# Second feed-forward product: sums in the places of blocks that are read no more, the late block in two buffers, operand loads over two groups, x1 of the tail in halves

## The chip, the cores and the metric

The kernel runs on one core of a Trainium2 chip. The metric is the device time of one execution in microseconds: before the change the median of three runs is 2979.29 us (2977.74 to 2981.48). Times inside an execution come from the hardware profiler's trace of one further execution; they count from its first instruction. Engines are named as in the profile: PE is TensorE, DVE VectorE, ACT ScalarE, POOL GpSimd, SP SyncE. SP and POOL issue DMAs here; each has its own queue.

## The reference, cut to what matters

The reference is one inference step of a one-layer encoder for T = 576 tokens (512 of a prompt, 64 of a sample) with D = 2048. After a token mixer that leaves x1, the change touches the feed-forward part:

```python
def conv_ffn(h, conv_prev, lp):
    ...
    up = h @ lp['w_up']
    ...
    out = (jax.nn.gelu(a_conv) * bv) @ lp['w_down']
...
f, conv_new = conv_ffn(h2, conv_prev, lp)
x = x + rms_norm(f, lp['norm_post_ffn'])
```

Here `w_up` is 2048 x 11264 and `w_down` 5632 x 2048, all in float32. The second product, gelu(a) * b times `w_down`, is called the down product below; its 5632 rows are the gated hidden channels.

## The kernel before, in words

**Float32 in three passes.** A weight block of 128 x 1024 numbers is loaded into a buffer `raw` (SP), cast into `wh` (ACT, L148: the high part, in a type that TensorE takes at full pace), and the rest raw - wh is written into `wl` by a subtraction (DVE, L160; every second block of the last eight on POOL). The operand has two parts too, `xh` and `xl`, prepared the same way and kept in DRAM (`gcd`). A product is three matmuls: wh with xh, wh with xl, wl with xh.

**One list of blocks.** All weight blocks stand in one list and `go(i)` works on block i. In the last parts of the kernel it issues loads some blocks ahead (`dma_to`), sees to the subtraction of block i + 1 (`l_to`), then the evacuations that the block before has left in `late`, then sums and the cast of block i + 2 (`h_to`), and last the 24 matmuls of block i. Each engine runs its own instructions in this order, and each DMA queue issues in its order too; an instruction that must wait holds everything behind it on its engine.

**The down product (L1530, PE).** 5120 of the 5632 rows are cut into five chunks, the 2048 columns into four quarters: 20 groups, number n = 4 * chunk + quarter. A group is a 2 x 2 block product by a seven-product scheme: weight blocks A11, A12, A21, A22 and sums of them, against seven operand combinations kept in SBUF (`E`, `xh`, `xl`, high and low halves). A group therefore has seven positions of 24 matmuls. In the order of work the weights are: A11; A12; A11 + A21 + A22; A21 + A22; A11 + A21; A11 + A12 + A21 + A22 combined in `ws1`; A22. Five of the sums are made by DVE (`tt`, L1537), all into two buffers `ws0` and `ws1`; the third position takes two sums, one on the other's result, made in a row ahead of its cast.

**Banks.** Three PSUM banks are used in a group, in the order A, B, A, C, A, C, A. The third position cannot start until the first one's bank has been evacuated into `f` (DVE, L1537; in chunk 0 four of the seven on ACT, L1960), the fourth use waits for the third, and so on.

**Loads.** A11, A21, A12 come into the three rotating `raw` buffers, in SP's queue. A22, the late block, has one buffer of its own; SP loads it (`w_load`, L1911) when the block at position 5 has been handed to PE. The operands of the next chunk lie in the other half of the SBUF operand buffers: 14 loads of 576 KB (`ring_load`, L1885), issued by POOL. In program order they stand in the second group of a chunk, high and low half of an operand together, but they wait only for the last matmul that reads what they overwrite, and that is in the last group of the chunk before: that is when they run.

**The up product's end.** The last group of the up product ends in `down_open`, which makes the last gating (two products on DVE and their stores), closes the buffers of the up product, opens those of the down product (`f`, `ws`) and issues the first load of A22.

**The tail (L1993).** The last 512 rows are a plain product of 16 blocks, eight for tokens 256 to 575 and eight for tokens 0 to 255. Between them `tail_square` collects squares, `tail_turn` (L2089) transposes and scales, and `tail_out` (L2131, `scalar_tensor_tensor` on DVE) adds x1 and stores. x1 comes from DRAM (`x1td`) in six loads on POOL's queue, all in `tail_start` (L2049, L2051).

Of the kernel before, what the change touches and what calls it, by code (L numbers as in the profile page):

```python
# [36 lines left out]
def kernel(ctx: ExitStack, tc: tile.TileContext, I: dict, O: dict):  # L37
# [1440 lines left out]
    def ffn_open():  # L1478
        M3["cm"].__exit__(None, None, None)
        rbc_.__exit__(None, None, None)  # L1480
        extra["pool"] = None
        F["ecm"] = tc.tile_pool(name="pe", bufs=1, reuse_waits="tile")
        F["ep"] = F["ecm"].__enter__()
        F["E"] = F["ep"].tile([P, 2, 3, 8, HT], F32R, tag="E", name="E")
        F["cm"] = tc.tile_pool(name="p4", bufs=1, reuse_waits="tile")
        p = F["cm"].__enter__()
        F["p"] = p
        extra.update(pool=p, n=2, kind=2, turn=4)
# [4 lines left out]
        F["a2"] = [p.tile([P, 578], F32, name="a%d" % j) for j in range(2)]  # L1493
# [4 lines left out]
        F["xt"] = p.tile([P, T], F32, name="xtok")  # L1498
        for k in range(2):
            x_load(k)  # L1500
# [53 lines left out]
    def x_step(p, n):  # L1554
# [5 lines left out]
        if n == 1:  # L1560
            tt(a0, a0, a1, ALU.subtract)
            tt(a1, b1, a1, ALU.subtract)
        elif n == 2:
            stt(b1, a0, -1.0, b1, ALU.subtract)
            nc.scalar.copy(E[:, 0, 0:2, p, :], x2)
        elif n == 3:
            stt(b0, b1, -1.0, b0, ALU.subtract)
            nc.scalar.copy(E[:, 0, 2, p, :], b1)
        elif n == 4:
            gh = F["gh", "x"] = F["p"].tile([P, T], F32R, tag="gh", name="gh", bufs=2)  # L1570
            nc.scalar.copy(gh[:, 0:HT], b0)
            nc.scalar.dma_start(x4d[0, :, p], gh[:, 0:HT].bitcast(F32))
            low(E[:, 1, 0:2, p, :], x2, E[:, 0, 0:2, p, :])
        elif n == 5:
            low(E[:, 1, 2, p, :], b1, E[:, 0, 2, p, :])
        elif n == 6:
            gl = F["p"].tile([P, T], F32R, tag="gl", name="gl")
# [184 lines left out]
    def xtok(k, step):  # L1762
# [19 lines left out]
        elif step == 5:  # L1782
            xo = F["p"].tile([P, T], F32, tag="gh", name="xo", bufs=2)
# [3 lines left out]
    def up_group(q, part):  # L1787
# [24 lines left out]
        def run(j):  # L1812
            def run_(h, lo):
# [37 lines left out]
                if last:  # L1851
                    ring_load(0, SEVEN[j])
                    if j == 3:
                        conv_last()
                    if j == 6:
                        while late:
                            late.pop(0)()
                        down_open(q)
# [8 lines left out]
    def conv_last():  # L1867
# [4 lines left out]
        co = F["p"].tile([P, T], F32, tag="gh", name="co", bufs=2)  # L1872
# [8 lines left out]
    def ring_load(c, o):  # L1881

        for hl in range(2):
# [6 lines left out]
    def down_open(q):  # L1890
# [5 lines left out]
        F["cm"].__exit__(None, None, None)  # L1896
        evp_.__exit__(None, None, None)
        extra["pool"] = None
        F["cm"] = tc.tile_pool(name="p5", bufs=1, reuse_waits="tile")
        F["p"] = F["cm"].__enter__()  # L1900
        F["f"] = [F["p"].tile([P, 4, T], F32, name="f%d" % m) for m in range(4)]
        F["ws"] = [F["p"].tile([P, 1024], F32, name="ws%d" % m) for m in range(2)]
        F["A22"] = stage_w["t"][2].bitcast(F32)
        w_load(F["A22"], 0, 0, 1, 1)
# [4 lines left out]
    def w_load(dst, c, mq, m, e):  # L1909

        nc.sync.dma_start(  # L1911
# [4 lines left out]

    def down_group(c, mq):
        R = {}

        def ld(name, m, e):  # L1920
            def load(alloc):
                R[name] = alloc()
                w_load(R[name], c, mq, m, e)
            return load

        def add(j, a, b):
            def src():
                g = lambda x: F["ws"][x] if isinstance(x, int) else F["A22"] if x == "A22" else R[x]
                tt(F["ws"][j], g(a), g(b), ALU.add)
                return F["ws"][j]  # L1930
            return src

        def two_sums():
            add(0, "A21", "A22")()
            return add(1, 0, "A11")()

        srcs = [lambda: R["A11"], lambda: F["ws"][0], two_sums, lambda: R["A12"],
                add(0, "A11", "A21"), add(1, 1, "A12"), lambda: F["A22"]]
        loads = [ld("A11", 0, 0), None, ld("A21", 1, 0), ld("A12", 0, 1), None, None, None]

        def run(j):
            def run_(h, lo):
# [29 lines left out]
        for j in (0, 3, 2, 1, 4, 5, 6):  # L1972
            block(1024, loads[j], run(j), srcs[j], 3)
# [4 lines left out]
    def last_run(a, mb):  # L1978
# [61 lines left out]
    def tail_start():  # L2040
# [11 lines left out]
        nc.scalar.activation(F["sp"].tile([P, 2], F32), ones, AF.Sqrt)  # L2052
# [82 lines left out]
    def tail_end():  # L2135
# [5 lines left out]
        F["cm"].__exit__(None, None, None)  # L2141
        F["ecm"].__exit__(None, None, None)
# [8 lines left out]
    def go(i):  # L2151
# [4 lines left out]
        else:  # L2156
            up = i < N_DOWN
            dma_to(i + 9 if i < N_DOWN - 9 else min(i + 9, N_DOWN + 6) if up else i + 7 if i < N_TAIL else i + 4)
# [3 lines left out]
            if up:  # L2162
                s_to(min(i + 3, N_DOWN))
                h_to(min(i + 2, N_DOWN))
# [89 lines left out]
```

## Time and profile before

| what | value |
|---|---|
| median of three runs | 2979.29 us (2977.74 to 2981.48) |
| the profiled execution's own time | 2983.06 us |
| its span, first to last instruction | 2981.3 us |
| mean granted TensorE clock | 0.984 |
| PE busy | 2847.2 us |
| DVE busy | 1844.2 us |
| ACT busy | 1171.7 us |
| POOL busy | 547.7 us |
| up product's last stretch | 1851.86 to 2339.71 us |
| down product | 2349.50 to 2885.80 us |
| tail | 2885.80 to 2981.30 us |

A window row gives the stretch, its length, the busy time and number of instructions of PE, PEld (weight loads into the array), DVE, ACT and POOL, then the granted clock, the busy share of the DMA engines and GB/s. A timeline row gives start, duration, engine, line, operation and tiles, and in brackets the idle time before it with what ended it. In the wait view a row gives the total, the number and the longest. "issue" is idle time for which the profile shows no cause. Matmuls overlap, so a matmul's duration of some 0.29 us is longer than the distance between two starts.

### The profile page before, as it was taken

What the parts mean: (1) busy time and instruction counts of PE and PEld (TensorE: products, weight loads), DVE (VectorE), ACT (ScalarE), POOL (GpSimd) and SP (SyncE); (2) the same over time, 40 slices, a digit from 0 to 9 for tenths busy, and PEclk for the clock granted to TensorE, in tenths of its full rate; (3) what the DMA queues carried; (4) which work ended last, traced back from release to release, by engine and by line L of the source; (5) the groups of instructions that cost most, each with busy time, mean ns of one, the idle gap of its engine ahead of it and who ended that gap; (6) DMA issues with size and microseconds to landing.
All of it is one profiled execution on the core that took longest, in us unless ns stands there. A gap on an engine that the chain in (4) does not pass through costs nothing.

```text
span 2981.3 us, 51790 instructions
## 1 busy us (share of the span) xinstructions
PE 2847.2 (96%) x21387; PEld 2783.9 (93%) x21387; DVE 1844.2 (62%) x2585; ACT 1171.7 (39%) x1764; POOL 547.7 (18%) x619
## 2 busy tenths in 40 slices
PE   8999999999999999998899999999999797898987
PEld 7999999999999999988899999999999797898986
DVE  7424533435252233378888888888888566676766
ACT  4322422222222234455555555555555342222223
POOL 2200010133330004454121211100000300110105
PEclk9999999999999999999999999999999899999998
DMA  8732343344343335574655554544544943543353
GB/s 272 195 79 68 83 129 81 99 112 113 98 115 98 96 120 156 163 234 158 196 161 155 175 164 147 160 136 128 160 137 126 321 143 132 196 164 110 117 162 129
DMA packets 519532, 431.51 MB, mean 145 GB/s; under 512 B 62844, under 2 KB 472114, under 8 KB 517952
## 3 DMA queue, kind: packets, MB, share of 16 engines
q1 hardware_dynamic: 467296, 298.42, 34.6%
q0 software_dynamic: 25792, 97.30, 9.5%
q10 hardware_dynamic: 26208, 32.48, 3.1%
q8 instruction: 168, 2.75, 0.4%
q14 instruction: 68, 0.56, 0.1%
HBM read 343.94 MB, written 84.90 MB: 144 GB/s over the span
## 4 chain that ended last, share of the span: by engine, by line
PE 80%; DVE 9%; DMA 4%; issue 3%; ACT 2%; POOL 1%; SPq 0%; ACTq 0%; DVEq 0%; POOLq 0%
PE ps L1530 37%; PE ps L199 36%; DVE wl L160 3%; DVE ws L1537 2%; DMA wl<-in_w_down_dram 2%; PE ps L224 2%; ACT wh L148 2%; DVE f L1537 1%; PE ps L327 1%; PE ps L1993 1%; DVE xl L1400 1%; DMA raw<-in_w_down_dram 1%; PE ps L1070 0%; PE ps L1074 0%; PE ps L622 0%
## 5 line engine op out<-in xcount | busy, mean ns | idle before, releaser
L160 DVE TENSOR_TENSOR wl<-raw,wh 128x1024 fp32r<-128x1024 f32 (+2 forms) x406 | 489.3, 1206 | 352.9 <-ACT wh L148 227.4
L1530 PE MATMUL ps<-E,wh 128*128 128x288 f32 x2880 | 589.2, 299 | 71.0 <-issue 32.4
L199 PE MATMUL ps<-xh,wl 128*128 128x288 f32 x2944 | 642.9, 296 | 13.7 <-DVE wl L160 13.7
L199 PE MATMUL ps<-xh,wh 128*128 128x288 f32 x2944 | 651.6, 299 | 3.7 <-DVE r_ss L1366 1.9
L199 PE MATMUL ps<-xl,wh 128*128 128x288 f32 x2944 | 641.7, 296 | 3.2 <-DVE xl L1400 3.2
L148 ACT CAST wh<-raw 128x1024 fp32r<-128x1024 f32 (+2 forms) x398 | 399.2, 1003 | 529.1 <-PE ps L199 290.2
L1530 PE MATMUL ps<-xh,wh 128*128 128x288 f32 x1920 | 569.4, 297 | 6.0 <-DVE f L1537 4.9
L1530 PE MATMUL ps<-xh,wl 128*128 128x288 f32 x1920 | 565.3, 294 | 0.7 <-DVE wl L160 0.7
L1530 PE MATMUL ps<-xl,wh 128*128 128x288 f32 x1920 | 565.1, 294 | 0.0
L1530 PEld LDWEIGHTS ps<-E,wh 128*128 128x128 f32 x2880 | 469.0, 191 | 74.7 <-issue 51.0
L199 PEld LDWEIGHTS ps<-xh,wl 128*128 128x128 f32 x2944 | 478.5, 189 | 16.0 <-DVE wl L160 15.8
L199 PEld LDWEIGHTS ps<-xh,wh 128*128 128x128 f32 x2944 | 476.8, 189 | 16.7 <-issue 9.9
L199 PEld LDWEIGHTS ps<-xl,wh 128*128 128x128 f32 x2944 | 478.2, 189 | 4.7 <-DVE xl L1400 4.7
L1530 PE MATMUL ps<-E,wl 128*128 128x288 f32 x1440 | 428.2, 297 | 0.4 <-DVE wl L160 0.4
L1530 PEld LDWEIGHTS ps<-xh,wh 128*128 128x128 f32 x1920 | 360.2, 188 | 9.6 <-issue 8.0
L1530 PEld LDWEIGHTS ps<-xh,wl 128*128 128x128 f32 x1920 | 360.2, 188 | 1.0 <-DVE wl L160 1.0
L1530 PEld LDWEIGHTS ps<-xl,wh 128*128 128x128 f32 x1920 | 360.3, 188 | 0.0
L1530 PEld LDWEIGHTS ps<-E,wl 128*128 128x128 f32 x1440 | 275.2, 191 | 1.0 <-DVE wl L160 1.0
L160 DVE TENSOR_TENSOR wl<-sums,wh 128x1024 fp32r<-128x1024 f32 x160 | 196.0, 1225 | 49.9 <-PE ps L1530 47.4
L148 ACT CAST wh<-ws 128x1024 fp32r<-128x1024 f32 x80 | 82.2, 1047 | 300.4 <-DVE ws L1537 277.2
L148 ACT CAST wh<-sums 128x1024 fp32r<-128x1024 f32 x160 | 168.2, 1051 | 62.7 <-PE ps L1530 59.6
L160 DVE TENSOR_TENSOR wl<-ws,wh 128x1024 fp32r<-128x1024 f32 x80 | 97.9, 1224 | 77.3 <-ACT wh L148 67.7
(464 smaller groups left out, 3037.0 us busy)
## 6 DMA issues: line engine op xcount, KB each, us to landing
raw<-in_w_up_dram SPq DMA_DIRECT2D x180, 512.0 KB
raw<-in_w_in_dram SPq DMA_DIRECT2D x118, 512.0 KB
raw<-in_w_down_dram SPq DMA_DIRECT2D x60, 512.0 KB
gcd<-gh ACTq DMA_DIRECT2D x62, 288.0 KB
E<-gcd POOLq DMA_DIRECT2D x30, 576.0 KB, 8.9
gd<-ev SPq DMA_DIRECT2D x48, 288.0 KB
gate<-gd SPq DMA_DIRECT2D x48, 288.0 KB
gcd<-wl POOLq DMA_DIRECT2D x40, 288.0 KB, 3.0
```

The costliest lines, as they stand in the source:

```text
L148: (nc.vector.tensor_copy if 4 <= i < KD else nc.scalar.copy)(as_src(raws[i], h, n), raws[i])
L160: E.tensor_tensor(out=out, in0=raw, in1=hi, op=ALU.subtract)
L199: mm(ps[:, a, 0:HT], w[:, c0:c0 + P], x[:, a * HT:(a + 1) * HT], start=start and i == 0, stop=stop and i == 2,)
L224: nc.tensor.transpose(out, in_, ident[0:k, 0:k])
L327: mm(mps[t][:, a, :], x[:, c], w[:, a * 512:(a + 1) * 512], start=k == 0 and i == 0, stop=k == KD - 1 and i == 2)
L1400: nc.vector.scalar_tensor_tensor(out=xl[:, k, c], in0=x1[:, c], scalar=gcol[:, G_FFN, k:k + 1], in1=xh[:, k, c].bitcast(F32), op0=ALU.mult ...
L1530: mm(bank, w[:, c0:c0 + P], x, start=start and p == 0 and i == 0, stop=p == n - 1 and i == 2, skip_group_check=True)
L1537: nc.vector.tensor_tensor(out=out, in0=a, in1=b, op=op)
L1993: mm(ps[:, j, 0:n], w[:, c], x, start=k == 0 and i == 0, stop=k == 3 and i == 2)
```

## The change

- **Sums in place.** Four sums a group instead of five, each made as soon as its inputs are there: at position 0 A11 += ws0 (ws0 holds A21 + A22), at position 2 ws0 = A11 + A12 (with what A11 has become), at position 5 ws0 = A21 + A22 of the next group, at position 6 A21 += A11 of the next group. Group 0 makes its first three at position 0. A sum stands behind the subtraction and the evacuations of its step.
- **The late block in two buffers**: the old one and `ws1`, alternating. The first A22 is loaded on POOL's queue during the last group of the up product.
- **Loads by name**: A22 of the next group at position 1, A21 and A11 at position 2, A12 at position 3, into buffers that are held, A21 and A12 swapping theirs from group to group.
- **Operand loads over two groups**: the high halves stand in the second group of a chunk, the low halves in the third.
- **The up product's end** is split: `down_open` opens only what the first group needs, and `up_close` makes the last gating at position 3 of the first group.
- **The tail**: a third `wl` buffer, subtractions one block earlier, the first raw blocks loaded in the last group, x1 in ten halves, one a block.

The core of the diff:

```diff
-        if kind < 2:
+        if kind < 2 or kind == 4:
             return wp.tile([P, 1024], F32R, tag="wl", name="wl", bufs=3)
...
                 if last:
+                    if j == 0:
+                        w_load(stage_w["t"][2].bitcast(F32), 0, "A22", nc.gpsimd)
                     ring_load(0, SEVEN[j])
...
-        F["f"] = [F["p"].tile([P, 4, T], F32, name="f%d" % m) for m in range(4)]
+        F["f"] = [F["p"].tile([P, 4, T], F32, name="f0")]
         F["ws"] = [F["p"].tile([P, 1024], F32, name="ws%d" % m) for m in range(2)]
-        F["A22"] = stage_w["t"][2].bitcast(F32)
-        w_load(F["A22"], 0, 0, 1, 1)
+        F["A22"] = (stage_w["t"][2].bitcast(F32), F["ws"][1])
...
+    def w_buf(n, name):
+
+        if name == "A22":
+            return F["A22"][n % 2]
+        return R5[0 if name == "A11" else 1 + n % 2 if name == "A21" else 2 - n % 2]
+
+    def down_sums(n, pos):
+
+        def s1(n):
+            tt(F["ws"][0], w_buf(n, "A21"), w_buf(n, "A22"), ALU.add)
+
+        def s3(n):
+            tt(w_buf(n, "A21"), w_buf(n, "A21"), w_buf(n, "A11"), ALU.add)
+
+        if pos == 0:
+            if n == 0:
+                s1(0)
+                s3(0)
+            tt(w_buf(n, "A11"), w_buf(n, "A11"), F["ws"][0], ALU.add)
+        elif pos == 2:
+            tt(F["ws"][0], w_buf(n, "A11"), w_buf(n, "A12"), ALU.add)
+        elif n + 1 < 4 * NCH and pos > 4:
+            (s1, s3)[pos - 5](n + 1)
+
+    def down_loads(n, pos):
+
+        if n + 1 < 4 * NCH:
+            for name in {1: ("A22",), 2: ("A21", "A11"), 3: ("A12",)}.get(pos, ()):
+                w_load(w_buf(n + 1, name), n + 1, name)
+        elif pos in (2, 3):
+            dma_to(N_TAIL + pos - 1)
...
-                if j == 5 and (c, mq) != (NCH - 1, 3):
-                    n = c * 4 + mq + 1
-                    w_load(F["A22"], n // 4, n % 4, 1, 1)
-                if mq == 1 and (c + 1 < NCH or j in (0, 3, 5, 6)):
-                    ring_load(c + 1, SEVEN[j])
+                down_loads(n, DOWN_ORDER.index(j))
+                if mq in (1, 2) and (c + 1 < NCH or j in (0, 3, 5, 6)):
+                    ring_load(c + 1, SEVEN[j], mq - 1)
+                if n == 0 and j == 1:
+                    up_close(NI // 2 - 1)
...
             if a == 0 and mb == 0:
                 tail_start()
+            elif a == 0 or mb < 3:
+                n_ = mb - 1 + 8 * a
+                x1_load((2, 3, 4, 0, 1)[n_ // 2], n_ % 2)
...
-        for t in range(4):
-            nc.gpsimd.dma_start(x1r(t, 0, D), x1td[t * P:(t + 1) * P, :])
-        for hf in range(2):
-            nc.gpsimd.dma_start(x1r(4, hf * 1024, 1024), x1td[512:576, hf * 1024:(hf + 1) * 1024])
...
+            elif i < N_TAIL:
+                h_to(i + 1)
+                l_to(i + 1)
+                down_sums((i - N_DOWN) // 7, (i - N_DOWN) % 7)
+                h_to(i + 2)
             else:
                 h_to(i + 1)
                 l_to(i + 1)
                 h_to(i + 2)
+                l_to(i + 2)
```

What stands on DVE, before, from position 0 of the third group of a chunk on (`wl<-` is a subtraction, `f1<-f1,ps` an evacuation, the rest are sums; `wl_14553` is A22):

```order
L160 TENSOR_TENSOR wl_14551<-raw_27306,wh_27467 128x1024
L1537 TENSOR_TENSOR f1_24492<-f1_24492,ps1_27279 128x2x288
L1537 TENSOR_TENSOR ws0_24495<-raw_27339,wl_14553 128x1024
L1537 TENSOR_TENSOR ws1_24496<-ws0_24495,raw_27271 128x1024
L160 TENSOR_TENSOR wl_14552<-ws1_24496,wh_27501 128x1024
L1537 TENSOR_TENSOR f2_24493<-f2_24493,ps0_27503 128x2x288
L160 TENSOR_TENSOR wl_14551<-ws0_24495,wh_27532 128x1024
L1537 TENSOR_TENSOR f2_24493<-f2_24493,ps1_27534 128x2x288
L1537 TENSOR_TENSOR ws0_24495<-raw_27271,raw_27339 128x1024
```

The two sums for the third position stand in a row; its subtraction (from `ws1`) and then the evacuation of the first position (`f2` from `ps0`) stand behind them. The same place after the change, from position 5 of the group before it on (`raw_24151` is A11, `raw_24153` A21, `raw_24155` A12, `wl_14556` A22):

```order
L1539 TENSOR_TENSOR ws0_24482<-raw_24153,wl_14556 128x1024
L160 TENSOR_TENSOR wl_14555<-raw_24151,wh_27398 128x1024
L1539 TENSOR_TENSOR f1_24626<-f1_24626,ps3_27339 128x2x288
L1539 TENSOR_TENSOR raw_24153<-raw_24153,raw_24151 128x1024
L160 TENSOR_TENSOR wl_14554<-raw_24155,wh_27428 128x1024
L1539 TENSOR_TENSOR f1_24626<-f1_24626,ps1_27246 128x2x288
L1539 TENSOR_TENSOR raw_24151<-raw_24151,ws0_24482 128x1024
L160 TENSOR_TENSOR wl_14555<-raw_24151,wh_27458 128x1024
L1539 TENSOR_TENSOR f2_24627<-f2_24627,ps0_27460 128x2x288
```

Three steps in a row now hold a subtraction, an evacuation and one sum each; one sum stands between the first position's subtraction and the third's.

POOL's operand loads of one chunk, before (`E`, `xh` and `xl` hold the operand combinations):

```order
L1885 DMA xh<-gcd 128x4x288
L1885 DMA xl<-gcd 128x4x288
L1885 DMA xh<-gcd 128x4x288
L1885 DMA xl<-gcd 128x4x288
L1885 DMA E<-gcd 128x1152 x6
L1885 DMA xh<-gcd 128x4x288
L1885 DMA xl<-gcd 128x4x288
L1885 DMA xh<-gcd 128x4x288
L1885 DMA xl<-gcd 128x4x288
```

After:

```order
L1892 DMA xh<-gcd 128x4x288 x2
L1892 DMA E<-gcd 128x1152 x3
L1892 DMA xh<-gcd 128x4x288 x2
L1892 DMA xl<-gcd 128x4x288 x2
L1892 DMA E<-gcd 128x1152 x3
L1892 DMA xl<-gcd 128x4x288 x2
```

The seven high halves now stand ahead of the seven low ones. A high half waits for the last matmul on its operand, which reads both halves, so a low half behind all seven has nothing left to wait for.

More of the change, by code (lines that the diff above doesn't have):

```diff
@@ L1492, in ffn_open @@
         F["a"] = [sa[:, j * 578:(j + 1) * 578] for j in range(4)]
-        F["a2"] = [p.tile([P, 578], F32, name="a%d" % j) for j in range(2)]
+        F["a2"] = [F["r"].tile([P, 578], F32, name="a%d" % j) for j in range(2)]
         for a in F["a"] + F["a2"]:
@@ L1879, with ring_load @@
     NP = 4
-    def ring_load(c, o):
-        for hl in range(2):
+    def ring_load(c, o, *hls_):
+        for hl in hls_ or range(2):
             if c < NCH:
@@ L1888, in ring_load, with down_open, up_close @@
                     nc.gpsimd.dma_start(opnd(o, hl, 4 + u).bitcast(F32), gcd[hl, o, :, q, :])
-    def down_open(q):
+    def down_open():
+        F["cm"].__exit__(None, None, None)
+        extra["pool"] = None
+        F["cm"] = tc.tile_pool(name="p5", bufs=1, reuse_waits="tile")
+        F["p"] = F["cm"].__enter__()
+        F["f"] = [F["p"].tile([P, 4, T], F32, name="f0")]
+        F["ws"] = [F["p"].tile([P, 1024], F32, name="ws%d" % m) for m in range(2)]
+        F["A22"] = (stage_w["t"][2].bitcast(F32), F["ws"][1])
+    def up_close(q):
         c0, c1 = F["c", 2 * q], F["c", 2 * q + 1]
@@ L1895, in down_open, with w_load @@
         g_plain(q)
-        F["cm"].__exit__(None, None, None)
+        F["rcm"].__exit__(None, None, None)
         evp_.__exit__(None, None, None)
-        extra["pool"] = None
-        F["cm"] = tc.tile_pool(name="p5", bufs=1, reuse_waits="tile")
-        F["p"] = F["cm"].__enter__()
-        F["f"] = [F["p"].tile([P, 4, T], F32, name="f%d" % m) for m in range(4)]
-        F["ws"] = [F["p"].tile([P, 1024], F32, name="ws%d" % m) for m in range(2)]
-        F["A22"] = stage_w["t"][2].bitcast(F32)
-        w_load(F["A22"], 0, 0, 1, 1)
+        F["fcm"] = tc.tile_pool(name="p6", bufs=1, reuse_waits="tile")
+        p = F["fcm"].__enter__()
+        F["f"] += [p.tile([P, 4, T], F32, name="f%d" % m) for m in range(1, 4)]
     def f_at(m):
         return F["f"][m // 4][:, m % 4, :]
-    def w_load(dst, c, mq, m, e):
-        nc.sync.dma_start(
+    def w_load(dst, n, name, queue=None):
+        c, mq, m, e = n // 4, n % 4, int(name[1]) - 1, int(name[2]) - 1
+        (queue or nc.sync).dma_start(
             dst.rearrange("p (j c) -> p j c", j=NP),
@@ L1915, in w_load, with first @@
         )
-    def down_group(c, mq):
[L1918 to L1939, printed above, removed]
+    R5 = []
+    DOWN_ORDER = (0, 3, 2, 1, 4, 5, 6)
+    def w_buf(n, name):
[22 more added lines that the diff above has]
+            dma_to(N_TAIL + pos - 1)
+    def down_group(c, mq):
+        n = c * 4 + mq
+        def first(alloc):
+            for name in ("A11", "A21", "A12"):
+                R5.append(alloc())
+                w_load(R5[-1], 0, name)
+        s1 = lambda: F["ws"][0]
+        srcs = [lambda: w_buf(n, "A11"), s1, lambda: w_buf(n, "A11"), lambda: w_buf(n, "A12"),
+                lambda: w_buf(n, "A21"), s1, lambda: w_buf(n, "A22")]
         def run(j):
@@ L1964, in run_ @@
                 late.append(evac)
-                if j == 5 and (c, mq) != (NCH - 1, 3):
-                    n = c * 4 + mq + 1
-                    w_load(F["A22"], n // 4, n % 4, 1, 1)
-                if mq == 1 and (c + 1 < NCH or j in (0, 3, 5, 6)):
-                    ring_load(c + 1, SEVEN[j])
-            return run_
-        for j in (0, 3, 2, 1, 4, 5, 6):
-            block(1024, loads[j], run(j), srcs[j], 3)
+                down_loads(n, DOWN_ORDER.index(j))
[3 more added lines that the diff above has]
+                    up_close(NI // 2 - 1)
+            return run_
+        for j in DOWN_ORDER:
+            block(1024, first if n == 0 and j == 0 else None, run(j), srcs[j], 3)
     PARTS = [(256, 320, (2, 3, 4)), (0, 256, (0, 1))]
@@ L2140, in tail_end @@
                 tail_out(1, i, hf)
-        F["cm"].__exit__(None, None, None)
-        F["ecm"].__exit__(None, None, None)
+        for cm in ("fcm", "cm", "ecm"):
+            F[cm].__exit__(None, None, None)
     n3 = KD + 8 + 2 * 65 + 6 + 48 + 3 * (KD - M_HALF)
@@ L2157, in go @@
             up = i < N_DOWN
[L2158 removed]
+            if up:
+                dma_to(min(i + 9, N_DOWN))
+            elif i >= N_TAIL:
+                dma_to(i + 4)
             l_to(min(i + 1, pos["h"] - 1))
```

27 lines of the change are left out of this document (17 added, 10 removed).

## The prediction

> **What bounds the kernel now.** The page of the profile comes first: TensorE is busy for nearly the whole span, so only two things can shorten it, less matmul work or shorter stops. The diff leaves every matmul in place, so I look for stops.
>
> ```profile
> span 2981.3 us, 51790 instructions
> PE 2847.2 (96%) x21387; PEld 2783.9 (93%) x21387; DVE 1844.2 (62%) x2585; ACT 1171.7 (39%) x1764; POOL 547.7 (18%) x619
> ```
>
> Second, the busy time by windows: the last stretch of the up product, the whole down product, one of its groups, the first and the second half of the tail.
>
> ```profile
> core 0: us, PE busy (x) PEld busy (x) DVE busy (x) ACT busy (x) POOL busy (x), PEclk, DMA share, GB/s
> 1851.86:2339.71 487.85, 487.85 (x3676) 487.84 (x3674) 429.00 (x503) 260.84 (x393) 48.09 (x97) 1.00 0.49 145
> 2349.50:2885.80 536.30, 462.04 (x3362) 454.91 (x3361) 345.91 (x346) 154.79 (x160) 48.35 (x77) 0.95 0.47 155
> 2805.84:2830.33 24.49, 22.79 (x168) 22.39 (x169) 17.73 (x19) 7.16 (x8) 0.00 (x0) 1.00 0.28 87
> 2885.80:2928.50 42.70, 35.95 (x236) 35.16 (x235) 22.59 (x43) 15.18 (x24) 18.95 (x19) 0.88 0.66 210
> 2928.50:2981.30 52.80, 33.91 (x252) 32.50 (x250) 37.86 (x70) 13.17 (x26) 26.93 (x18) 0.86 0.40 136
> ```
>
> The first row is the pace without stops: 487.85 / 3676 = 0.1327 us a matmul, 3.185 us a block of 24, 22.3 us a group of seven. The down product's 140 blocks would take 445.9 us at that pace and take 536.3: **90.4 us are lost**. Third, TensorE's waits from 2349.5 on, and fourth, pieces of the chain that ended last:
>
> ```profile
> PE ps L1530 <- issue: 32.8, 5, 12.2
> PE ps L1530 <- DVE f L1537: 20.4, 24, 1.3
> PE ps L1530 <- ACT f L1960: 19.7, 1, 19.7
> PE ps L1993 <- POOL wl L160: 6.9, 3, 2.4
> ```
>
> ```profile
> 2360.87 12.32 DMA wl<-in_w_down_dram
> 2457.95 17.91 DMA wl<-in_w_down_dram
> 2567.20 15.13 DMA wl<-in_w_down_dram
> 2674.90 16.28 DMA wl<-in_w_down_dram
> 2887.69 19.49 DMA raw<-in_w_down_dram
> ```
>
> The four `wl` pieces are loads of the late block A22. The first is the 19.7 us stop at the opening; the next three are the long stops that the wait view puts down to nothing ("issue"), one of them shown here with the small stops of a group (2818.52 is the last matmul ahead of one):
>
> ```profile
> 2481.52 0.82 PE L1530 MATMUL ps<-E,wh 128*128 128x288 f32 x2 [12.21 <-issue]
> 2818.52 0.29 PE L1530 MATMUL ps<-xh,wl 128*128 128x288 f32 x1
> 2820.10 0.50 PE L1530 MATMUL ps<-E,wh 128*128 128x288 f32 x2 [1.29 <-DVE f L1537]
> 2830.33 0.37 PE L1530 MATMUL ps<-xh,wh 128*128 128x288 f32 x1 [0.41 <-DVE f L1537]
> ```
>
> So the loss splits: a group costs 24.49 - 22.3 = 2.19 us too much; chunk 0 sends evacuations to ScalarE, so 16 groups pay, 35.0 us. The opening is 19.7. The rest, 90.4 - 35.0 - 19.7 = 35.7, goes to three late blocks, 11.9 each.
>
> **The sums: 35.0 us removed, 3.2 added.** VectorE from position 0 of a group on, and ScalarE's cast behind the two sums (start, duration, what ended the idle time before):
>
> ```profile
> 2812.58 1.23 DVE L160 TENSOR_TENSOR wl<-raw,wh 128x1024 fp32r<-128x1024 f32 x1 [1.31 <-issue]
> 2813.72 0.75 DVE L1537 TENSOR_TENSOR f<-f,ps 128x576 f32<-128x576 f32 x1
> 2814.39 1.22 DVE L1537 TENSOR_TENSOR ws<-raw,wl 128x1024 f32<-128x1024 f32 x1
> 2815.64 1.23 DVE L1537 TENSOR_TENSOR ws<-ws,raw 128x1024 f32<-128x1024 f32 x1
> 2816.98 2.00 ACT L148 CAST wh<-ws 128x1024 fp32r<-128x1024 f32 x2 [6.74 <-DVE ws L1537]
> 2818.06 1.22 DVE L160 TENSOR_TENSOR wl<-ws,wh 128x1024 fp32r<-128x1024 f32 x1 [1.19 <-ACT wh L148]
> 2819.20 0.75 DVE L1537 TENSOR_TENSOR f<-f,ps 128x576 f32<-128x576 f32 x1
> ```
>
> Two dependent sums, the cast, the subtraction and only then the evacuation for which TensorE waits until 2820.10. One sum is now made earlier, so all behind it comes 2815.64 - 2814.39 = 1.25 us sooner: restart at 2818.85. Unhindered it would have been one matmul (0.13) after the last start, 2818.52, so 2818.65: 0.2 us a group stay. The second stop (0.41) has the same chain at position 5; its sum now stands three blocks ahead. VectorE's steps with a sum take 1.14 + 0.67 + 1.14 = 2.95 us by the distances of the starts (3.06 with the dependent distance 1.25), under 3.185, also three in a row; five sums become four. So 16 x 0.2 = 3.2 us, between 0 and 16 x 1.29 = 21 if VectorE runs a sum late.
>
> **The late block: 55.4 us removed, about 2 added.** Before, A22 has one buffer; its load starts when the last block that reads it is split, two blocks (6.4 us) before its next use. Alone that is enough: issued at 2831.35, landed before 2835, so 3.7 us:
>
> ```profile
> 2831.35 0.37 SPq L1911 DMA_DIRECT2D wl<-in_w_down_dram  x1
> 2835.00:2836.00 1.00, 1.00 (x9) 1.00 (x9) 0.76 (x2) 0.00 (x0) 0.00 (x0) 1.00 0.00 0
> ```
>
> The 12 to 18 us come when POOL's 14 operand loads of the next chunk (8.26 MB) fill the DMA engines; here are the two queues from 2440 to 2482 (packets, MB), SP's own issues, and three full microseconds:
>
> ```profile
> q0 software_dynamic: 2016, 8.26, 54.8%
> q1 hardware_dynamic: 2112, 2.10, 14.9%
> 2450.20 4.20 SPq L1911 DMA_DIRECT2D raw<-in_w_down_dram  x3
> 2459.00:2462.00 3.00, 3.00 (x24) 3.00 (x24) 1.89 (x2) 0.00 (x0) 1.52 (x2) 1.00 1.03 398
> ```
>
> SP's four loads, 2.10 MB, took from 2450.2 to 2457.95 + 17.91 = 2475.9: 82 GB/s of 398, or 6.4 us a load inside a burst.
>
> After, A22 alternates between two buffers; its load is released seven blocks (22 us) before its use, longer than any landing above: the stops go. What is late next? A block starts 0.3 us before its first subtraction (2818.65 - 2 x 3.185 = 2812.28, against 2812.58), so its sum starts 2.1 us in and ends 3.3 us in. A21 and A11 of the next group are loaded when the sum at position 2 has read the old blocks. A21 is wanted by the sum at position 5: 3 x 3.185 + 2.1 - 3.3 = 8.4 us later. A11 is wanted by a cast that starts 1.08 us ahead of the subtraction at position 6: 4 x 3.185 + 0.3 - 1.1 - 3.3 = 8.6 us. A12 has some 10. Seven of the operand loads now follow TensorE block by block (0.59 MB in 3.185 us, 185 GB/s; with four 0.52 MB weight blocks a group, 94 GB/s, that is well below 398), and seven go at once when the group ends: 4.13 MB / 398 GB/s = 10.4 us. A21 and A11 are asked for 2 x 3.185 + 3.3 = 9.7 us into the next group, so 0.7 us of burst is left: no stop. In the opening the 14 loads of chunk 1 still go at once, behind the last stores of the up product, and the A21 and A11 of group 2 fall near the burst's end: I put 1 us on that, 0 to 5.
>
> A rule speaks against that margin. The Trainium skill, "DMA: Bandwidth & Descriptors", section "Queues, rings and completion order", says that a DMA engine turns from one queue row to the next packet by packet, so shares go by packets and not by bytes. The trace agrees: 2016 packets of 4 KB beside 2112 of 1 KB, one for one, a fifth of the bytes for SP. With even shares of bytes, 199 GB/s, a load in a burst would take 2.6 us and any burst would be harmless; by the rule it matters whether the burst outlives 9.7 us. The sum is 451 by both; the second rival is the case in which they part.
>
> The opening's stop goes too: A22 of group 0 is loaded on POOL's queue during the last group of the up product, behind a store and ahead of chunk 0's operand loads, which it delays by some 3 us; they have a whole group of 22 us. Group 0 makes three sums in a row: 1.0 us of stop, 0 to 3. The last gating of the up product moves behind its position 3, beside TensorE; uncovered it would cost two VectorE products, some 2 x 0.75 = 1.5 us. Down product: 445.9 + 3.2 + 1.0 + 1.0 = 451.
>
> **The tail: 14 us removed.** Six loads of x1 at the tail's start hold up a raw block; the second fence has pieces of the chain, with their number of matmuls:
>
> ```profile
> 2907.28 1.04 ACT L148 CAST wh<-raw 128x1024 fp32r<-128x1024 f32 x1 [12.11 <-DMA raw<-in_w_down_dram]
> 2908.38 0.64 PE L1993 MATMUL ps<-xh,wh 128*128 128x320 f32 x1 [6.39 <-ACT wh L148]
> 2940.72 2.35 POOL L160 TENSOR_TENSOR wl<-raw,wh 128x1024 fp32r<-128x1024 f32 x1
> 2941.16 3.00 DVE L2131 SCALAR_TENSOR_TENSOR et<-et,xl 128x1024 f32<-128x1024 f32 x1
> ```
>
> ```profile
> 2909.64 4.63 PE ps L1993 x16
> 2915.29 3.52 PE ps L1993 x24
> ```
>
> The stop is 6.4 us, and behind it a matmul takes 4.63 / 16 = 0.289 instead of 3.52 / 24 = 0.147 us (the clock of that half is 0.88), 24 x 0.142 = 3.4 more: 10 together, which halves spread over ten steps (one 0.5 MB load per 4 us beside a 0.5 MB block) give back; bounds 6 to 12. The three waits on POOL's subtraction (6.9 us) shrink as it starts one block earlier in a third buffer. But VectorE is busy 37.86 of the last 52.80 us and slows beside POOL (3.00 where a sum of that size takes 1.22): I take 4, 0 to 6.9. Tail: 95.5 - 14 = 81.5.
>
> **Sum.** 2349.5 + 451 + 81.5 = 2882 us of span, 99 less. The profiled execution took 2983.06, 1.8 more than its span and 3.8 more than the median 2979.29; so the median is forecast at 2979.3 - 99 = **2880 us**. Some 0.2%, 6 us, can be told from no change.
>
> **The rivals.** *VectorE runs a sum late* in each group, as its margin of 0.13 to 0.24 us a step is small: 16 x 1.29 - 3 = 18 more, 2898. For: no row has three such steps in a row. Against: the distances above. 0.14.
>
> *The burst outlives the margin*: operand loads start late or the low halves take longer, A21 and A11 meet them at a fifth of the rate, 2 x 6.4 - 8.6 = 4.2 us late per chunk, 17 over four chunks; priced by the rows of before, 4 x 11.9 = 48: 2897 to 2928. 0.09.
>
> *Slower*: every group stops, since A21 now has 8.4 us where before raw blocks were asked for seven positions ahead. Were each landing 17.9 us, as the worst row, 20 groups lose 9.5 each, 190: 3070. It turns the gain when the mean landing passes 8.4 + 99/20 = 13.4 us. Against: 3.7 us alone, and the engines idle half the time (share 0.47). 0.03.
>
> *It doesn't do what it says at the opening*: A22 on POOL's queue waits for its store, chunk 0's operands slide, and the 19.7 us stay: 2900. 0.05.
>
> **How the numbers follow.** The forecast has 0.69: 2880 with 0 to 12 (sums), 0 to 7 (opening) and -5 to +8 (tail), about 2872 to 2895. The range 2868 to 2905 takes in the first and the last rival and half of the second, and leaves out the rest. All but the slower one are faster by far more than 6 us: faster 0.96, same 0.01, slower 0.03.
>
> **What would show it.** Right: no late-block load in the chain, groups of 22.5 us, TensorE's waits in the down product under 10 us in all, the clock there 0.99, the tail's first half without the 12 us wait of the cast. Wrong: stops behind `raw<-in_w_down_dram` at positions 5 and 6 (loads), stops of 1 us behind `f` at position 2 (VectorE), a stop near 2350 (opening).

## The result and the profile after

The changed kernel takes 2898.95 us in the median of four runs (2896.91 to 2899.85), the kernel before 2978.51 (2972.55 to 2981.48): a ratio of 0.9734, with a 95% interval of 0.9718 to 0.9751. That is 79.6 us faster, where 99 were forecast; the time lies inside the range that was given, 19 us above the number, and outside the 2872 to 2895 us that the prediction worked out for its own forecast.

The page of the profile after:

```profile
span 2898.1 us, 51797 instructions
PE 2837.4 (98%) x21387; PEld 2775.3 (96%) x21387; DVE 1843.7 (64%) x2585; ACT 1174.1 (41%) x1764; POOL 547.4 (19%) x624
```

VectorE's busy time and its number of instructions are what they were (1844.2 us, x2585): the kernel before makes four sums a group too, not five, as the texts above say by mistake (no term of the forecast hangs on that count). The change only puts them elsewhere. What changed is how long TensorE stands still. Its waits from 2345 us on:

```profile
PE ps L1532 <- ACT wh L148: 3.8, 1, 3.8
PE ps L1532 <- DVE f L1539: 3.5, 5, 0.8
PE ps L224 <- DVE f L2041: 3.1, 5, 0.9
PE ps L2033 <- POOL wl L160: 2.3, 2, 1.2
PE ps L1532 <- ACT f L1997: 1.9, 1, 1.9
```

The 32.8 us of "issue" and the 19.7 us behind ScalarE are gone, the 20.4 us behind VectorE are 3.5. The windows of the same execution: the start of the down product up to the first operand load that TensorE paces, a steady group, two groups across a chunk border, the whole down product, and the two halves of the tail:

```profile
2347.78:2430.84 83.06, 75.21 (x534) 73.84 (x533) 52.85 (x50) 31.98 (x38) 13.09 (x20) 0.96 0.72 247
2502.45:2525.02 22.57, 22.54 (x168) 22.34 (x169) 17.68 (x18) 7.26 (x8) 0.75 (x1) 1.00 0.36 109
2525.02:2571.89 46.87, 45.52 (x337) 44.76 (x337) 35.70 (x37) 15.32 (x15) 8.48 (x13) 1.00 0.76 260
2347.78:2814.51 466.73, 455.17 (x3362) 450.14 (x3361) 347.85 (x348) 156.72 (x160) 49.85 (x79) 0.99 0.55 180
2814.51:2849.91 35.40, 33.75 (x237) 32.38 (x235) 23.92 (x43) 15.01 (x24) 13.58 (x19) 1.00 0.63 196
2849.91:2898.10 48.19, 32.48 (x252) 31.04 (x250) 34.71 (x70) 13.48 (x27) 29.71 (x23) 0.86 0.55 186
```

A group takes 22.57 us where it took 24.49. The down product takes 466.7 us instead of 536.3; its 140 blocks at the full pace are 445.9, so 20.8 are still lost, and 13.0 of them before 2430.84: that moment is the end of its 22nd block, which was due at 2347.78 + 22 x 3.185 = 2417.85. The chain that ended last names what is waited for there and at two chunk borders:

```profile
2331.52 18.71 DMA raw<-in_w_down_dram
2386.20 14.88 DMA raw<-in_w_down_dram
2551.22 10.29 DMA raw<-in_w_down_dram
2643.22 9.49 DMA raw<-in_w_down_dram
```

None of them is the late block. The first is A12 of group 0. The other three are A11, the second of three loads issued together: of group 2, and at two chunk borders. Each ends where ScalarE's cast of the block starts. TensorE's stops that belong to the first two:

```profile
2351.74 0.40 PE L1532 MATMUL ps<-xh,wh 128*128 128x288 f32 x1 [0.64 <-ACT a L1851]
2352.82 0.40 PE L1532 MATMUL ps<-xl,wh 128*128 128x288 f32 x1 [0.68 <-DMA xl<-gcd]
2357.97 0.53 PE L1532 MATMUL ps<-E,wh 128*128 128x288 f32 x2 [1.86 <-ACT f L1997]
2402.27 0.40 PE L1532 MATMUL ps<-xh,wh 128*128 128x288 f32 x1 [3.76 <-ACT wh L148]
2403.53 0.52 PE L1532 MATMUL ps<-xh,wl 128*128 128x288 f32 x1 [0.73 <-DVE wl L160]
```

### The profile page after: what moved, and what is told of

It is laid out like the page before. It is cut to its first block, busy times and chain, and to the rows that moved or that the text cites. A ratio compares the mean times of both kernels' runs of the same rounds, so it can differ in the third digit from the quotient of the medians.

```text
span 2898.1 us, 51797 instructions
## 1 busy us (share of the span) xinstructions
PE 2837.4 (98%) x21387; PEld 2775.3 (96%) x21387; DVE 1843.7 (64%) x2585; ACT 1174.1 (41%) x1764; POOL 547.4 (19%) x624
## 4 chain that ended last, share of the span: by engine, by line
PE 87%; DVE 6%; DMA 3%; issue 2%; ACT 1%; POOL 1%; SPq 0%; DVEq 0%; ACTq 0%; POOLq 0%
PE ps L1532 43%; PE ps L199 38%; DMA raw<-in_w_down_dram 2%; PE ps L224 2%; DVE wl L160 2%; DVE xl L1400 1%; PE ps L327 1%; ACT wh L148 1%; PE ps L1070 0%; PE ps L1074 0%; PE ps L622 0%; PE ps L656 0%; DMA raw<-in_w_mem_kv_dram 0%; DMA a<-x1d 0%; DVE raw L1539 0%
## 5 line engine op out<-in xcount | busy, mean ns | idle before, releaser
L160 DVE TENSOR_TENSOR wl<-raw,wh 128x1024 fp32r<-128x1024 f32 (+2 forms) x446 | 542.0, 1216 | 339.5 <-ACT wh L148 259.6
L148 ACT CAST wh<-raw 128x1024 fp32r<-128x1024 f32 (+2 forms) x438 | 441.2, 1007 | 661.3 <-PE ps L199 289.8
L1532 PE MATMUL ps<-E,wh 128*128 128x288 f32 x2880 | 581.3, 296 | 6.3 <-DVE f L1539 2.5
L1532 PEld LDWEIGHTS ps<-E,wh 128*128 128x128 f32 x2880 | 462.0, 188 | 9.7 <-issue 5.6
L1186 ACT COPY ev<-ps 128x576 f32<-128x576 f32 x48 | 30.7, 640 | 272.9 <-PE ps L199 272.9
L1539 DVE TENSOR_TENSOR sums<-raw 128x1024 f32<-128x1024 f32 x80 | 97.5, 1218 | 0.3 <-DMA raw<-in_w_up_dram 0.3
```

The source lines that it names most:

```text
L148: (nc.vector.tensor_copy if 4 <= i < KD else nc.scalar.copy)(as_src(raws[i], h, n), raws[i])
L160: E.tensor_tensor(out=out, in0=raw, in1=hi, op=ALU.subtract)
L1186: nc.scalar.copy(halves(e), ps[:, :, 0:HT])
L1532: mm(bank, w[:, c0:c0 + P], x, start=start and p == 0 and i == 0, stop=p == n - 1 and i == 2, skip_group_check=True)
L1539: nc.vector.tensor_tensor(out=out, in0=a, in1=b, op=op)
```

## The experiments

Every kernel below is the changed kernel with one edit, unless it says otherwise. Times are medians of four runs (five for the last), beside runs of the kernel before that stayed between 2978.0 and 2979.1 us in every group of runs, so they are compared with the changed kernel's 2898.95. The four runs of one kernel lie 2 to 7 us apart, so differences under some 4 us are not told apart by the times alone.

### Operand loads together again

```diff
-                if mq in (1, 2) and (c + 1 < NCH or j in (0, 3, 5, 6)):
-                    ring_load(c + 1, SEVEN[j], mq - 1)
+                if mq == 1 and (c + 1 < NCH or j in (0, 3, 5, 6)):
+                    ring_load(c + 1, SEVEN[j])
```

> The changed kernel, but the high and low half of an operand are again loaded together, in one group (the two late buffers stay). Theory (the split keeps the weight loads out of the burst): 14 loads paced by TensorE ask for 370 GB/s beside 94 GB/s of weights, more than the 398 seen, so a backlog stands in the DMA engines when a chunk begins, and A21 and A11 of its next groups land late: 4 to 12 us at each of the three later chunk borders, 2911 to 2935 us. Rival (the two late buffers alone cured it): within 2 us of the changed kernel's 2899.

Measured: 2922.57 us (ratio 0.9812, 0.9797 to 0.9826), 23.6 slower. Its waits in the down product, of TensorE:

```profile
PE ps L1532 <- ACT wh L148: 12.7, 4, 5.7
PE ps L1532 <- DMA xh<-gcd: 4.5, 1, 4.5
```

The waits behind ScalarE's cast are four instead of one: raw blocks land late, and in one place the operands themselves. Two late buffers alone do not cure the borders.

### The kernel before, with the operand loads split

The same split in the kernel before, nothing else:

```diff
-                if mq == 1 and (c + 1 < NCH or j in (0, 3, 5, 6)):
-                    ring_load(c + 1, SEVEN[j])
+                if mq in (1, 2) and (c + 1 < NCH or j in (0, 3, 5, 6)):
+                    ring_load(c + 1, SEVEN[j], (mq - 1,))
...
```

> The kernel before, with one thing changed: operand loads over two groups, high halves first. Theory (the stops on the late block come from the burst, not from its single buffer): the three stops inside the down product, 11.9 us each, go, the opening's 19.7 us and the 2.19 us a group stay: 33 to 36 us faster than before, about 2943 us. Rival (one buffer is too late by itself): at most 10 us faster.

Measured: 2947.11 us (ratio 0.9891, 0.9877 to 0.9906), 31.4 faster than before. Its waits:

```profile
PE ps L1530 <- DVE f L1537: 20.3, 24, 1.3
PE ps L1530 <- ACT f L1960: 18.0, 1, 18.0
PE ps L1530 <- issue: 6.6, 8, 1.2
```

The three long stops are gone with one late buffer; what is left under "issue" are eight of the small stops (at most 1.2 us). So inside the down product the stops on the late block came from the burst, and the second buffer was not needed against them. That is shown at this kernel's 24.5 us a group; one buffer with the split at the changed kernel's 22.57 us was not tried. The opening's 18.0 us and the 24 stops behind VectorE stay.

### A sum made twice, at position 5

```diff
-            tt(F["ws"][0], w_buf(n, "A21"), w_buf(n, "A22"), ALU.add)
+            for _ in range(2 if n else 1):
+                tt(F["ws"][0], w_buf(n, "A21"), w_buf(n, "A22"), ALU.add)
```

> The changed kernel with the sum at position 5 made twice (the second writes the same values). Theory (VectorE has no slack left where three sums stand in a row): the three steps take 3 x 2.95 + 1.25 = 10.1 us against 9.56 of TensorE, so the chain behind position 0 starts 0.6 to 1.2 us late and TensorE stops that much longer in each of 16 groups: 8 to 20 us slower, 2907 to 2919. Rival (VectorE is well ahead there): within 2 us of 2899.

Measured: 2906.10 us (ratio 0.9754, 0.9738 to 0.9771), 7.2 slower, a little under the theory's range. A group of this kernel:

```profile
2572.04:2595.35 23.31, 22.55 (x168) 22.34 (x169) 18.73 (x20) 7.18 (x8) 0.00 (x0) 1.00 0.31 91
```

1.22 us of work more cost 0.74 us a group: VectorE had some 0.5 us of slack over its three steps with a sum, and not more. Over 16 groups that would be 11.8 us; the total is less for two reasons that the trace shows. At the chunk borders part of the extra work falls into the wait for the loads: two such groups take 23.84 and 23.39 us here, 24.09 and 24.34 in the changed kernel. And group 0 was 4.1 us shorter in this execution (24.16 against 28.25).

### Two products in a row, at position 0

```diff
+            tt(w_buf(n, "A11"), w_buf(n, "A11"), w_buf(n, "A11"), ALU.max)
             tt(w_buf(n, "A11"), w_buf(n, "A11"), F["ws"][0], ALU.add)
```

> The changed kernel with one more VectorE product of the same size at position 0, ahead of the sum there and on the same block (the greater of A11 and A11, which leaves it as it is): again two dependent products in a row ahead of the cast of the third position, and five of them a group. Theory (what cost 2.19 us a group before was the row of two, not the number of sums): the third position starts 1.25 us later in the 16 groups of chunks 1 to 4, whose first evacuation is on VectorE, 18 to 22 us slower than the changed kernel, about 2919 us; the groups of chunk 0 lose less. Rival (it is the amount of work on VectorE): about what the sum made twice at position 5 cost, 7 us, 2906.

Measured: 2918.19 us (ratio 0.9799, 0.9783 to 0.9816), 19.2 slower. A group, and TensorE's stop at its start:

```profile
2576.05:2599.88 23.83, 22.55 (x168) 22.34 (x169) 18.90 (x20) 7.15 (x7) 0.00 (x0) 1.00 0.29 89
```

```profile
2576.05 0.50 PE L1532 MATMUL ps<-E,wh 128*128 128x288 f32 x2 [1.29 <-DVE f L1539]
```

The stop of 1.29 us is back, the very one of the kernel before, and the group takes 23.83 us, 1.26 more than the changed kernel's. The same length of work costs 0.74 us a group at position 5 and 1.26 at position 0, where the cast of the third position stands behind it: the place in the chain decides first, the amount of work second. The theory's 18 to 22 us hold.

### Chunk 1's operand loads spread, on ScalarE's queue

```diff
-                nc.gpsimd.dma_start(opnd(o, hl, 4 * (c % 2), NP).bitcast(F32), ...
+                q_ = nc.scalar if c == 1 else nc.gpsimd
+                q_.dma_start(opnd(o, hl, 4 * (c % 2), NP).bitcast(F32), ...
```

> The changed kernel, but the 14 operand loads of chunk 1 are issued by ScalarE in its own order, one a block, instead of by GpSimd at once. Theory (in the opening this burst, started by the last stores of the up product, holds up A21 and A11 of group 2): the stop of 3.8 and 0.7 us near 2402 us and the slow clock behind it go, 6 to 7 us faster than the changed kernel, about 2892 us. Rival (those weight loads are late by themselves, because their buffers come free late): within 2 us of 2899.

Measured: 2892.89 us (ratio 0.9708, 0.9692 to 0.9724), 6.1 faster, as the theory had it; the stops at 2402 us are gone. In the changed kernel GpSimd and SP had issued:

```profile
2367.19 1.10 POOL L1672 DMA_DIRECT2D gcd<-xtok  x2 [13.38 <-DVE xtok L1539]
2430.84 0.75 POOL L1892 DMA_DIRECT2D xh<-gcd  x1 [44.06 <-PE ps L1532]
```

```profile
2385.72 1.72 SPq L1925 DMA_DIRECT2D raw<-in_w_down_dram  x3
```

The stores wait for the last gating until 2367, the 14 loads of chunk 1 stand behind them and are issued until 2386 and land 11 to 14 us after their issue, and the three raw blocks of group 2, asked for at 2385.72, fall into that. The two queues from 2390 to 2395, while both have loads under way:

```profile
q0 software_dynamic: 382, 1.57, 81.3%
q1 hardware_dynamic: 376, 0.39, 22.1%
```

As many packets of the one as of the other, four times the bytes. The edit both spreads the loads and moves them to another queue; this run does not part the two.

### The later chunks' operand loads there too

The same with `c == 1` replaced by `c`, so that chunks 1 to 4 go through ScalarE's queue. The operands of the last 512 rows stay on GpSimd's; that holds for the last experiment too, whose expectation says "chunks 1 to 5".

> As the kernel with chunk 1 on ScalarE's queue, but with all later operand loads there too, one a block over two groups, so that no burst is left. Theory: the losses at the later chunk borders (1.7 and 0.9 us) go as well, about 2890 us. Rival: ScalarE's issues delay its casts, or the spread loads slow each weight load a little in every group: slower than the kernel with chunk 1 alone, 2893 us or more.

Measured: 2886.66 us (ratio 0.9693, 0.9678 to 0.9707), 12.3 faster. Two groups across a chunk border:

```profile
2561.11:2606.22 45.11, 45.08 (x336) 44.66 (x337) 35.54 (x36) 14.49 (x15) 0.00 (x0) 1.00 0.81 265
```

The border, 46.87 us in the changed kernel, costs nothing any more, at a DMA share of 0.81. The 6.2 us beyond the edit for chunk 1 alone are more than the 1.7 and 0.9 us of the expectation, for two reasons. The border of chunks 0 and 1 loses 1.3 us in the changed kernel too, also behind late raw blocks. And in the trace of the kernel with chunk 1 alone on that queue the three borders cost more: two groups there take 47.30, 46.71 and 46.19 us, here 44.90, 45.11 and 45.10, 5.1 us less in all. Most of the rest lies in group 0 (28.71 and 27.07 us), which this edit does not touch.

### The first sums of group 0 earlier

```diff
+        tt(F["ws"][0], w_buf(0, "A21"), w_buf(0, "A22"), ALU.add)
+        tt(w_buf(0, "A21"), w_buf(0, "A21"), w_buf(0, "A11"), ALU.add)
     (at the end of down_open, and no longer at position 0)
```

> The changed kernel, but the first two sums of group 0 are made before VectorE's subtraction of A12, which waits for a late load. Theory (at the opening three sums queue behind that subtraction): the third position starts on time, 2 to 4.5 us faster than the changed kernel, about 2896 us. Rival (A21 or A22 of group 0 land no earlier than A12): within 1.5 us of 2899.

Measured: 2897.40 us (ratio 0.9727, 0.9713 to 0.9742), 1.6 faster: too little to tell apart by the times. VectorE at the opening of the changed kernel, and then of this one:

```profile
2351.41 1.23 DVE L160 TENSOR_TENSOR wl<-raw,wh 128x1024 fp32r<-128x1024 f32 x1 [4.32 <-ACT wh L148]
2352.55 1.22 DVE L1539 TENSOR_TENSOR ws<-raw,wl 128x1024 f32<-128x1024 f32 x1
...
2355.07 1.23 DVE L1539 TENSOR_TENSOR raw<-raw,ws 128x1024 f32<-128x1024 f32 x1
```

```profile
2346.06 1.22 DVE L1539 TENSOR_TENSOR ws<-raw,wl 128x1024 f32<-128x1024 f32 x1
2347.31 1.23 DVE L1539 TENSOR_TENSOR raw<-raw 128x1024 f32<-128x1024 f32 x1
2350.17 1.22 DVE L160 TENSOR_TENSOR wl<-raw,wh 128x1024 fp32r<-128x1024 f32 x1 [1.63 <-PE ps L1532]
```

The two sums run while VectorE would have waited for A12, and the stop of 1.86 us at the third position is gone. How much of that is the edit is open, since A12 lands at another time in every execution. In the kernel with x1 at once, whose opening is that of the changed kernel, VectorE waited 1.59 us for the cast of A12 instead of 4.32, the stop was 0.55 us, and group 0 took 24.01 us instead of 28.25; here it took 23.94. The three sums behind a late A12 cost the stop; with A12 nearly on time they cost little.

The stop in group 2 grows from 3.76 to 4.65 us. GpSimd's stores ahead of the burst and SP's loads for group 2:

```profile
2361.92 1.11 POOL L1672 DMA_DIRECT2D gcd<-xtok  x2 [10.35 <-DVE xtok L1539]
2380.46 2.07 SPq L1927 DMA_DIRECT2D raw<-in_w_down_dram  x3
```

Both come 5.3 us earlier than in the changed kernel (2367.19 and 2385.72), so they stand 18.5 us apart as before, and the blocks fall into the burst as before.

### x1 at once

```diff
-            elif a == 0 or mb < 3:
-                n_ = mb - 1 + 8 * a
-                x1_load((2, 3, 4, 0, 1)[n_ // 2], n_ % 2)
...
+        for t in range(4):
+            nc.gpsimd.dma_start(x1r(t, 0, D), x1td[t * P:(t + 1) * P, :])
+        for hf in range(2):
+            nc.gpsimd.dma_start(x1r(4, hf * 1024, 1024), x1td[512:576, hf * 1024:(hf + 1) * 1024])
```

> The changed kernel with x1 loaded again at once, in six loads at the tail's start. Theory of the prediction (these loads hold up a raw block of the tail, a stop of 6.4 us and 3.4 us of slow clock behind it): 8 to 10 us slower than the changed kernel, about 2908 us. Rival (with the first raw blocks loaded ahead in the last group, the burst has passed before a raw block is missed): within 2 us of 2899.

Measured: 2906.20 us (ratio 0.9759, 0.9746 to 0.9773), 7.3 slower. A stop of 7.2 us stands in the tail again, behind a cast that waits 7.76 us for a raw block of `w_down`:

```profile
PE ps L224 <- DVE f L2038: 9.2, 4, 7.2
```

### The tail's subtraction in its old place

```diff
-        if kind < 2 or kind == 4:
+        if kind < 2:
...
                 h_to(i + 2)
-                l_to(i + 2)
```

> The changed kernel, but the tail's subtraction is made one block later again and into two buffers as before. The prediction's step (the earlier subtraction shortens the waits on GpSimd): 4 us slower, 2903. Rival, from the trace after (blocks of the tail's first half take 5.02 us because VectorE's subtraction now stands ahead of the additions, behind a cast that waits for the squares of those additions, a ring of 5 us): the first half's blocks return to 4.18 us, 3.4 us faster there, the two waits on GpSimd of 1.1 and 1.2 us grow back to some 2.3 each: net between 3 us faster and 2 slower.

Measured: 2902.61 us (ratio 0.9740, 0.9725 to 0.9754), 3.7 slower, near the prediction's 4, though one of the four runs, 2897.87, was no slower than the changed kernel. The two halves of the tail show that both theories are at work:

```profile
2815.91:2848.69 32.78, 32.78 (x237) 32.73 (x235) 22.63 (x44) 15.21 (x24) 19.10 (x20) 1.00 0.66 210
2848.69:2901.50 52.81, 33.87 (x252) 32.45 (x250) 37.83 (x70) 13.34 (x26) 28.30 (x22) 0.83 0.53 176
```

Against the changed kernel's 35.40 and 48.19 us the first half is 2.6 faster and the second 4.6 slower. The ring in the first half of the changed kernel, VectorE and then ScalarE:

```profile
2835.08 1.69 DVE L160 TENSOR_TENSOR wl<-raw,wh 128x1024 fp32r<-128x1024 f32 x1 [1.54 <-ACT wh L148]
...
2837.69 0.87 DVE L2041 TENSOR_TENSOR f<-ps,f 128x320 f32<-128x320 f32 x2
```

```profile
2838.25 0.47 ACT L2144 ACTIVATE ws<-f 128x320 f32<-128x320 f32 x1 [3.20 <-DVE f L2041]
...
2839.03 1.03 ACT L148 CAST wh<-raw 128x1024 fp32r<-128x1024 f32 x1
```

The addition into `f` stands behind the subtraction, the squares behind the addition, the cast behind the squares, and the next subtraction waits for the cast: once round in 5.02 us. With the subtraction in its old place the casts of the first half come every 4.18 us.

### The earlier subtraction in the second half only

```diff
-                l_to(i + 2)
+                if i >= N_TAIL + 8:
+                    l_to(i + 2)
```

> The changed kernel, but in the tail the subtraction is made a block earlier only from the ninth block on, where GpSimd makes every second one. Theory (the earlier subtraction closes a ring of 5.02 us through VectorE and ScalarE in the first half, and pays only on GpSimd): the tail's first half as in the kernel with the late subtraction, 32.8 us, its second half like the changed kernel's or better: 3 to 5 us faster than the changed kernel, about 2895 us. Rival (the ring is as dear in the second half): within 1.5 us of 2899.

Measured: 2897.47 us (ratio 0.9730, 0.9716 to 0.9745), 1.5 faster: inconclusive by the times. In its trace the first half is back at 32.8 us, but a new stop of 2.1 us behind `f` stands where the order changes over.

### The earlier subtraction on GpSimd only

```diff
-                l_to(i + 2)
+                if i % 2 and i >= N_TAIL + 9:
+                    l_to(i + 2)
```

> The changed kernel, but in the tail only the blocks that GpSimd subtracts are subtracted a block earlier; VectorE's stand where they stood before. Theory (on VectorE the earlier place closes the ring of 5.02 us and adds stops behind f, on GpSimd alone it pays): tail's first half 32.8 us, no stop of 2.1 us behind f in the second, GpSimd's waits near 1.2 us each: tail 78 to 81 us against 83.4, 3 to 5 us faster, about 2895 us. Rival (what is gained on VectorE is lost on GpSimd): within 1.5 us of 2899.

Measured: 2893.98 us (ratio 0.9717, 0.9703 to 0.9730), 5.0 faster. Its tail:

```profile
2812.32:2845.10 32.78, 32.78 (x236) 32.73 (x235) 21.49 (x43) 15.20 (x24) 19.10 (x20) 1.00 0.61 199
2845.10:2891.20 46.10, 30.89 (x252) 29.47 (x250) 35.57 (x70) 13.09 (x26) 27.28 (x22) 0.91 0.59 202
```

78.9 us in all against 83.6: both halves gain, so the earlier place helps on GpSimd and harms on VectorE.

### Three of these together

ScalarE's queue for chunks 1 to 4, the first sums of group 0 earlier, the tail's earlier subtraction on GpSimd only.

> The changed kernel with three edits together: all operand loads of chunks 1 to 5 on ScalarE's queue, one a block; the first two sums of group 0 ahead of the subtraction of A12; the tail's earlier subtraction on GpSimd only. If the three losses are separate they add: 12.3 + 1.6 to 3 + 3 to 5 us, 2879 to 2882 us. If they cover each other: near 2886.7, the best of them alone.

Measured: 2879.63 us in the median of five (2876.16 to 2881.90; ratio 0.9667, 0.9654 to 0.9681), 19.3 faster than the changed kernel. The single gains, 12.3 + 1.6 + 5.0 = 18.9, add up within the scatter of the runs: nothing speaks for losses that cover each other. The longest waits of TensorE that are left from 2340 us on; two of 0.5 and 0.2 us are all in the down product, the first of them here:

```profile
PE ps L2033 <- DVE wl L160: 2.0, 2, 1.2
PE ps L224 <- DVE f L2041: 1.5, 2, 0.9
PE ps L2033 <- POOL wl L160: 1.2, 1, 1.2
PE ps L1532 <- DMA xl<-gcd: 0.5, 1, 0.5
```

## Why the prediction was right, and where its size was off

The time lies in the range, but not for the reason that the range was made wide. The forecast's own terms gave 2872 to 2895; the bound of 2905 was set to take in the first and the last rival and half of the second. The first and the last did not happen: a group loses 0.27 us and not the 1.29 of a late sum, and the stop of 19.7 us on A22 at the opening is gone. Of the second, the burst that outlives the margin, came 3.9 us at three borders, where 17 was its least. What fills the space above all is the opening, whose term was too small. So the mechanism of the gain is right, and that 2899 lies inside is in part luck. Of the signs that were named, TensorE's waits in the down product come to 11.4 us where under 10 stood.

Where the 2898.1 us of span stand against the 2882 that were forecast:

| term | forecast | trace after |
|---|---|---|
| start of the down product | 2349.5 | 2347.8 |
| 140 blocks at the full pace | 445.9 | 445.9 |
| opening, up to 2430.84 | 2.0 (0 to 8) | 13.0 |
| sums | 3.2 | 3.9 |
| chunk borders | 0 | 1.3 + 1.7 + 0.9 |
| tail | 81.5 | 83.6 |

- **The late block** (55.4 us removed): right in sum. No A22 is left in the chain. But the three inner stops went by the split of the operand loads, which alone gives 31.4 us in the kernel before (35.7 were put down to them); the second buffer was not what they needed. What took away the 19.7 us at the opening (the earlier load on POOL's queue, the second buffer, the split end of the up product) no run tells apart.
- **What is late next**: right in kind, not in "no stop". A21 and A11 are what is late at the chunk borders, and A11 binds. A21 is asked for at 2550.76, and its sum starts at 2560.11, 0.75 us after VectorE was free: a margin of 8.6 us where 8.4 were worked out. A11 lands 1.4 us later still, 10.3 us after its own issue, against a margin of 8.6 in the prediction. The burst outlives the margin by little, not by the 4.2 us of the second rival; putting the halves together again costs 23.6 us, within that rival's 17 to 48.
- **The sums** (35.0 removed, 3.2 added): right. 0.27 us a group is left of 2.19 (22.57 - 22.3) against 0.2 forecast, and the row of two brings its stop of 1.29 us back.
- **The opening**: here lies most of the error, and it is one of size. The terms are "I put 1 us on that, 0 to 5", for A21 and A11 of group 2 in the burst of chunk 1, and "1.0 us of stop, 0 to 3" for the three sums: 2.0 together, and 13.0 measured. In this trace some 6 of them lie in group 0, 28.25 us long. The three sums stood behind the subtraction of A12, which landed 18.71 us after its issue, in the operand loads of chunk 0; TensorE stopped 1.86 us for that, with slow clock behind it (0.53 from 2359.2 to 2362.8). This part differs from one execution to the next (24.01 us in the one with x1 at once). The rest is the burst: a stop of 3.76 us, another of 0.73, and slow clock again (0.93 in group 2). The stores ahead of the burst were issued at 2367.19, and A21 and A11 of group 2 were asked for 18.5 us later, at 2385.72. The 8.26 MB kept the DMA engines full until about 2400 (share 1.04 from 2375 to 2400), so the two blocks did not fall near the burst's end but some 14 us before it. The lateness of A12 did not cause that: with the first sums earlier the distance is 18.5 us too. The step had given the burst no start. Spreading it, on ScalarE's queue, gives 6.1 us back.
- **The tail** (14 forecast, 95.5 - 83.6 = 11.9 measured): x1 in halves is worth 7.3 us instead of 10. The earlier subtraction is worth 2.0 (trace) to 3.7 us (times) instead of 4, but as the sum of 4.6 won and 2.6 lost: the prediction saw the busy VectorE as the limit, not the ring through ScalarE.

The rule on the queues that the prediction weighed, from the Trainium skill, "DMA: Bandwidth & Descriptors", section "Queues, rings and completion order", agrees with the traces, but not by the counts that the prediction gives for it: 2016 and 2112 packets are simply all that the 14 operand loads and the four weight loads consist of, in whatever order they went. What bears on it is a stretch inside the burst, in which both queues have loads under way. In the kernel before, from 2455 to 2470:

```profile
q0 software_dynamic: 1153, 4.73, 81.2%
q1 hardware_dynamic: 1150, 1.14, 21.9%
```

Packets go one for one, and SP's queue gets 1.14 of 5.87 MB, a fifth. The 382 beside 376 packets of the changed kernel say the same.

## What to carry to other kernels

A buffer's load that lands late is a question of what else is in the DMA engines, before it is one of buffers: spreading the operand loads cured the stops that looked like a missing second buffer. When an instruction is moved ahead on an engine that serves several chains, walk once round the ring it closes (who waits for it, and what it waits for) and compare that time with the pace of the bound engine. And a burst must be dated in the changed program, by what now stands ahead of it in its queue.

## What the runs showed of the hardware

- The same operand loads go in smaller packets on ScalarE's queue than on GpSimd's. On GpSimd's they were of 4.1 KB (8.26 MB / 2016 in the kernel before). In the kernel with chunks 1 to 4 on ScalarE's queue, from 2460 to 2505, they were of 6.83 MB / 3962 = 1.7 KB on average, in a mixture: 0.61 MB / 150 = 4.1 KB from 2475 to 2480, 0.87 MB / 782 = 1.1 KB from 2485 to 2490. Part of what that kernel gains may come from this and not from the spreading; no run tells the two apart.
- The same subtraction of 128 x 1024 on VectorE took 1.22 us in the down product and 1.69 us in the tail's first half of the changed kernel (at 2835.08), where it began while GpSimd was in an addition (2834.82) that took its usual 0.87 us. In the kernel with the subtraction in its old place it took 1.21 us in the same half (at 2833.08), and GpSimd's addition, which began while it ran (2833.47), took 1.55 us. So in both cases the one that began first kept its length and the other grew. x1 was loaded in both stretches, so these loads alone are not the reason; no run was made for this alone.
